# Four of sixteen scale and shift columns of a hybrid decoder layer, computed on TensorE instead of VectorE

## The chip, the core and the metric

One core of a Trainium2 chip runs the whole layer in one launch. The metric is the device time of that launch in microseconds (us). PE is TensorE's matmul row and PEld its weight loads, DVE is VectorE, ACT is ScalarE, POOL is GpSimd, SP is SyncE, which here issues nearly all transfers.

## What is computed

The layer normalises the residual stream `x` (1024 tokens by 1024 channels), modulates it by a scale and a shift that come from a conditioning vector `c`, projects it, runs sparse attention and a state-space mixer side by side, and projects back. The change touches the modulation alone:

```python
mod = jax.nn.silu(c) @ w_ada + b_ada                # c: (1, 1024), w_ada: (1024, 3072)
shift, scale, gate = jnp.split(mod, 3, axis=-1)     # 1024 values each
h = rms_norm(x, norm_g) * (1 + scale[:, None, :]) + shift[:, None, :]
proj = h @ w_in
```

`silu(c) @ w_ada` is a product of one row with a matrix: 24 parts of 128 outputs, each over 1024 inputs. Parts 0 to 7 are the shift, 8 to 15 the scale, 16 to 23 the gate.

## The kernel before

**The parts of the modulation.** `mod_chunk(j)` (L230) loads 128 rows of the transposed `w_ada` (512 KB: one output on each partition, its 1024 weights along it) into a `w4` buffer and forms the sum on DVE: one `scalar_tensor_tensor` (the helper at L148) multiplies the tile by `sc` and adds up along the partition into one column of `macc`. `sc` holds `2 * silu(c)` copied to all 128 partitions; `sc_half` (L222) makes it from a 4 KB row by products with a column of ones (L224), a tanh on ACT (L225) and a step on DVE. The steps `ma0` to `ma7` are parts 8 to 15 (scale), `mb0` to `mb7` parts 0 to 7 (shift), `mod0` to `mod7` parts 16 to 23 (gate, needed much later).

**From the parts to h.** `mod_cols(k)` (step `mc{k}`, L286) turns the columns 8+k and k of `macc` into `gs` and `sh`, the gain and the shift of the 128 channels of block k. Meanwhile the tokens are prepared in two halves of 512: squares and their sums (`sq0` to `sq7`, the table `FLG` puts `sq0` and `sq3` on DVE, L148, the others on ACT, L242), the root (`rstd0`, `rstd1`: eleven small DVE instructions), the scaling of x (`xsc0`, `xsc1`: two tiles on DVE at L155, two on ACT at L257), and transposes on PE into PSUM (`xb{k}{half}`, L265, two buffers of tag `pv`). `h_chunk` (step `h{k}{half}`, L290) then runs two ACT instructions on that PSUM tile (L296), once into `hhi` in a reduced format, once into `hf` in full, and the remainder `hlo = hf - hhi` is formed on DVE, on POOL or by an accumulating transfer (L300). The sixteen h steps feed the first projections on PE: `kva{k}` (L330 to L332, three products per tile: high times high, high times low, low times high) and `u{k}m` (L351), which accumulate over k. `kvaw{k}` loads and splits the weights of `kva`: a cast on ACT (L208), a subtraction on DVE or POOL.

**Order.** A list of step names, `ORD`, gives the order in which the steps are written down. Its head is `sc1 sc0 lb pu xl_0 sq0 sq2 sq1 sq3 ma7 mb4 ma0 rstd0 mb0 kvaw0 ma5 xl_1 xsc0 sq5 xb10 sq4 xb00 sq6 sq7 mg mc0 h00 mb2 rstd1 xsc1 ma1 kvaw1 mb1 mc1 mb3 ma2 mc2 kvaw5 mb6 ...`. The context `in_order` (L170) pins that order on DVE and ACT up to the step `eo`, and on SP up to `sw`; what is written after `eo` may be placed earlier by the framework's scheduler where it finds an engine free, and PE and POOL are not pinned at all. Within an engine the program that comes out is fixed and is executed strictly in its order.

**Buffers.** `w4` has 19 buffers of 4 KB a partition and serves the weight tiles of `w_ada`, the squares' scrap tiles and the projection weights; SP holds back a load until the buffer it was given is released. In PSUM the tag `mm` has two buffers; the step `pu` takes both at the start for the accumulators `pu0` of `u{k}m`.

Of the kernel before, what the change touches and what calls it, by code (L numbers as in the profile page):

```python
# [26 lines left out]
ORD = """
sc1 sc0 lb pu xl_0 sq0 sq2 sq1 sq3 ma7 mb4 ma0 rstd0 mb0 kvaw0 ma5 xl_1 xsc0 sq5 xb10 sq4 xb00 sq6 sq7 mg mc0 h00 mb2
rstd1 xsc1 ma1 kvaw1 mb1 mc1 mb3 ma2 mc2 kvaw5 mb6 xb01 kvaw2 ma3 mc3 h01 xb20 mb5 eo kvaw4 mb7 h10 xb30 cU1 cz4 cU0
h20 xb21 h30 kvaw3 xb11 h11 h21 xb31 kvaw6 xb40 h31 ma4 s5l mc4 h40 xb70 mc7 ll h70 xb50 u0m u1m ma6 u2m mc5 h50 kva0  # L30
mc6 kva1 xb51 kva2 u3m xb61 xb60 h51 h61 xb71 h60 kva3 xb41 tb h41 kva4 kvaw7 h71 s5p u4m kva5 kva6 u5m kva7 u6m sw
tabf kpa0 kpa1 cKC kpan0 kvb0 kvb1 kvb2 prep0 kvb3 kvb4 kvb5 u7m u0 cU2 kvb6 mats0 xl0 kpat0 tab0 prep1 scan0 kpan1 u1
cU3 mats1 kpat1 xl1 kvb7 kpb0 tq kpb1 kpbn0 u2 qaw0 u3 mod0 mod1 out0 prep2 tab1 cVC kpbn1 scan1 out1 tab2 xl2 cmpk
qaw1 cmpv kpbt0 qaw2 qa0 mod2 mod3 mod4 mats2 hidk qaw3 qaw4 qaw5 qa1 qa2 kpbt1 qa3 qa4 qa5 mod5 qaw6 qa6 mod6 qaw7
qa7 qp0 qp1 qpn0 qs0 prep3 qpn1 qs1 tab3 hidv xl3 qw0 scan2 qr0 cz0 mats3 qw1 scan3 qb0 qb1 gw gates mod7 modf cok cov
cmpK qb2 scalev qb3 z0_0 z0_1 qb4 z0_2 qt01 qb5 qb6 qb7 out2 cz2 qr1 qt00 g2 cz1 z0_3 qpb0 qpb1 qpbn0 ca0 z0_4 qpbn1
z0_5 z0_6 z0_7 out3 cz3 kt ha00 ha01 hs01 hb00 hc00 ha02 z1_0 z1_1 z1_2 ha03 hs03 hb01 hb02 z1_3 z1_4 qsb0 z1_5 z1_6
hc01 ha04 qt10 ha05 hs05 hb03 hc02 hc03 hb04 hb05 z1_7 hc04 hc05 z2_0 yp00 z2_1 qsb1 ca1 ha06 ha07 hs07 hb06 z2_2 z2_3
z2_4 hb07 ct0 hc06 ha10 z2_5 hc07 z2_6 ub00 qt11 z2_7 ub01 ha11 hs11 hb10 hb11 ub02 z3_0 z3_1 z3_2 hc10 hc11 yp01 ha12
ha13 ub03 qw2 ct1 z3_3 qr2 ub04 ub05 ha14 ub06 ha15 cz5 z3_4 z3_5 ub07 ub10 z3_6 z3_7 hs15 hs13 hb12 hb13 z4_0 hb14  # L40
hb15 qt20 ub11 ha16 ha17 hc12 hc13 hc14 yp02 z4_1 z4_2 qt21 ub12 hs17 hb16 ha20 ha21 hb17 z4_3 ca2 hc15 hs21 ha22 z4_4
ha23 hc16 z4_5 z4_6 z4_7 hb20 ub13 cz6 hb21 hc17 hs23 hc20 yp03 ub14 yp10 z5_0 z5_1 z5_2 hb22 z5_3 qw3 qr3 ub15 hc21
z5_4 cz7 z5_5 z5_6 ha24 hb23 ha25 ub16 ub17 hs25 hb24 z6_0 z5_7 hc22 hc23 hc24 ha26 ha27 ct2 hs27 z6_1 z6_2 qt30 z6_3
z6_4 z6_5 z6_6 yp11 z6_7 yp12 hb25 hb26 hc25 ha30 qt31 ha31 ha32 ha33 hs31 hs33 ca3 hb27 hb30 z7_0 ub20 hc26 hb31 glul
z7_1 z7_2 z7_3 hb32 hc27 z7_4 z7_5 hc30 hc31 hc32 ha34 hb33 yp13 ub21 qw7 ha35 hs35 z7_6 z7_7 sp hc33 ct3 glu00 grow
ha36 ha37 glu03 qr7 qt70 hb34 hc34 glu01 qt71 ha70 ub22 ub23 ub24 ub25 hb35 hc35 ub26 hs37 ub27 hb36 hc36 ca7 ha71 ct7
glu02 glu10 glu11 hs71 ub30 hb37 hb70 qw6 glu12 qr6 ha72 ub31 ub32 ub33 hc37 hc70 at0 ha73 hs73 glu13 wo10 wo11 hb71
hc71 hb72 hc72 ha74 hb73 wo12 wo13 ub34 ub35 ub36 ha75 hc73 qt60 ub37 ub70 hs75 ha76 hb74 hb75 ha77 hs77 ub71 so0 so1
qt61 hc74 hc75 hb76 hb77 ca6 ub72 hc76 hc77 ha60 ha61 ct6 qw5 hs61 ub73 hb60 hc60 ub74 hb61 ha62 ha63 so2 hs63 qr5
hb62 ub75 ha64 hc61 hc62 hb63 ha65 ub76 hs65 hb64 hb65 ha66 ha67 so4 ub77 ca5 ub60 ub61 hc63 hc64 so5 qt50 ha50 qt51  # L50
ub62 hs67 hb66 hb67 hc65 qw4 qr4 ub63 so7 hc66 ha51 hs51 hc67 ub64 hb50 hb51 hc50 hc51 so6 ha52 ha53 ha54 ha55 ha56
hs53 ub65 hb52 hb53 ub66 so3 wo00 wo01 wo02 wo03 ct5 hc52 qt41 at3 hc53 ub67 ub50 hs55 hb54 hb55 hc54 ha57 hs57 ca4
ao30 hc55 hb56 hb57 ao31 ao00 ao01 qt40 at1 ha40 at2 ao10 ha41 hc56 hs41 hb40 hb41 hc57 hc40 ha42 ub51 ao11 ha43 ub52
ao20 hs43 hb42 hb43 ct4 hc41 hc42 ao21 ub53 ub54 ha44 ha45 at7 ub55 ub56 ub57 ao70 hc43 hs45 hb44 hb45 ao71 ha46 ub40
at5 at6 ha47 hc44 ao50 ao51 ao61 hs47 hc45 hb46 hc46 hb47 ao60 ub41 ub42 ub43 hc47 ub44 ub45 ub46 ub47
""".split()
FLG = dict(
    cw1280="d", cw1408="d", cw1536="d", cw1664="d", cw1816="d", cw1944="d", cw2072="d", cw2200="d", cw2328="d",
    cw2456="d", cw512="d", cw640="d", h00="p", h01="d", h10="p", h11="t", h20="p", h21="d", h30="d", h31="d", h40="d",
    h41="t", h50="t", h51="t", h60="d", h61="d", h70="t", h71="d", kw0="p", kw1="d", kw2="p", kw3="d", kw4="d",  # L60
    kw5="p", kw6="p", kw7="d", prep0="d", prep1="p", prep2="p", prep3="d", pw0="d", pw1="d", pw2="d", pw3="d",
    qw0="d", qw1="d", qw2="d", qw3="d", qw4="d", qw5="d", qw6="t", qw7="d", sq0="d", sq1="a", sq2="a", sq3="d",
    sq4="a", sq5="a", sq6="a", sq7="a", tab0="d", tab1="d", tab2="d", tab3="d", tabf="d", so0="p", at0="p", ao00="d",
    ao01="d", so1="d", at1="p", ao10="d", ao11="d", so2="p", at2="p", ao20="d", ao21="d", so3="d", at3="p", ao30="d",
    ao31="d", so4="d", ao40="d", ao41="d", so5="d", at5="p", ao50="d", ao51="d", so6="d", at6="p", ao60="d", ao61="d",
    so7="p", at7="d", ao70="d", ao71="d", wo00="d", wo01="d", wo02="d", wo03="d", wo10="d", wo11="d", wo12="d",
    wo13="d", xa0="d", xa1="d", xa2="t", xa3="d", xa4="d", xa5="d", xa6="d", xa7="d")
# [1552 lines left out]
```

## Time and profile before

| | |
|---|---|
| time, median of 3 runs | 692.42 us (692.40 to 692.64) |
| the profiled execution: its own time | 691.38 us |
| the profiled execution: span from first to last instruction | 689.5 us |
| PE busy | 623.5 us, 90% of the span |
| DVE busy | 567.3 us, 82% |
| ACT busy | 377.9 us, 55% |
| POOL busy | 148.6 us, 22% |
| granted TensorE clock, mean over the span | 0.980 |

The profile is of one execution. A busy share is a mean over stages with different limits, so the stage that the change touches (the first 60 us or so) is read by itself: the engines' instructions in order of time, with the idle time ahead of each and what ended it.

### The profile page before, as it was taken

The page shows a single profiled execution, that of the slowest core. Times are in us where ns is not written, and L with a number is a line of the kernel's source. Part 1 is how long each engine was busy: PE and PEld are TensorE (multiplying, and loading weights), DVE is VectorE, ACT ScalarE, POOL GpSimd, SP SyncE. Part 2 cuts the span into 40 slices and gives each one's busy share as a digit, 9 for nine tenths or more (in the row PEclk, how much of TensorE's full clock was granted, in tenths as well). Part 3 has the DMA queues.
Part 4 walks back from the last instruction along what each step waited for, and adds up shares of the span by engine and source line. Part 5 has one row for each costly group of instructions (what it writes and reads, how often), then busy time and mean ns, then how long its engine had stood idle before and what let it go on. Part 6 is the DMA issues. An engine that isn't in the chain of part 4 may idle for free.

```text
span 689.5 us, 12618 instructions
## 1 busy us (share of the span) xinstructions
PE 623.5 (90%) x4662; PEld 492.1 (71%) x4662; DVE 567.3 (82%) x1106; ACT 377.9 (55%) x732; POOL 148.6 (22%) x159
## 2 busy tenths in 40 slices
PE   2478999999698999999999999989899999799996
PEld 0356787788587886888788887556677777687775
DVE  5998999777937889876677787998898998998872
ACT  3677413735162252555586786547756855756640
POOL 0153209147232020640011101132001220011010
PEclk9989999999899999999999999999999999999999
DMA  8975211355276624373656868499689599688994
GB/s 319 417 246 104 47 62 41 115 158 136 64 246 199 212 68 109 83 231 94 131 139 154 207 186 183 124 207 208 183 172 206 132 226 222 184 215 213 224 222 86
DMA packets 209759, 116.76 MB, mean 169 GB/s; under 512 B 159073, under 2 KB 188513, under 8 KB 209698
## 3 DMA queue, kind: packets, MB, share of 16 engines
q1 hardware_dynamic: 205858, 109.38, 61.5%
...
q14 instruction: 24, 0.20, 0.1%
...
## 4 chain that ended last, share of the span: by engine, by line
PE 41%; DVE 21%; issue 5%; ACT 4%; DMA 2%; SPq 1%; POOL 1%; DVEq 0%; ACTq 0%; POOLq 0%
PE pcp L351 9%; PE po L1053 8%; PE S L1170 7%; DVE hl L148 4%; PE po L1263 3%; PE pglu L1015 3%; DVE st L1187 3%; PE ptp L331 2%; PE ptp L332 2%; PE ptp L330 1%; DVE ps L151 1%; ACT pp L1203 1%; DVE z L151 1%; PE pg L530 1%; PE ph L901 1%
## 5 line engine op out<-in xcount | busy, mean ns | idle before, releaser
L1203 ACT ACTIVATE pp<-S,st 128x640 f32<-128x640 f32 (+7 forms) x128 | 88.6, 699 | 60.5 <-DVE st L1187 46.5
L148 DVE SCALAR_TENSOR_TENSOR hl<-pp,st,hl 128x640 f16<-128x640 f32 (+7 forms) x128 | 100.5, 817 | 4.9 <-ACT hl L1222 4.8
L1222 ACT ACTIVATE hl<-pp,st 128x640 f16<-128x640 f32 (+7 forms) x128 | 85.2, 728 | 8.2 <-DVE st L151 7.1
L1053 PE MATMUL po<-wo,oh 128*128 128x512 f32 x264 | 85.2, 407 | 3.7 <-DVE wo L151 2.4
L351 PE MATMUL pcp<-hhi,wh 128*128 128x512 f32 x208 | 84.8, 408 | 0.0
L351 PE MATMUL pcp<-hhi,wl 128*128 128x512 f32 x208 | 82.6, 397 | 0.0
L351 PE MATMUL pcp<-hlo,wh 128*128 128x512 f32 x208 | 82.4, 396 | 0.0
L1187 DVE TENSOR_REDUCE st<-S 128x1 f32<-128x1024 f32 (+3 forms) x64 | 57.5, 916 | 6.9 <-PE S L1170 6.7
L1170 PE MATMUL S<-kT,qh 128*128 128x128 f32 (+3 forms) x192 | 60.7, 375 | 1.0 <-ACT pp L1203 0.7
L1053 PEld LDWEIGHTS po<-wo,oh 128*128 128x128 f32 x264 | 48.7, 191 | 14.9 <-DVE wo L151 3.8
L330 PE MATMUL ptp<-wsp,hhi 128*128 128x512 f32 x128 | 53.5, 420 | 6.5 <-ACT hhi L296 4.1
L1263 PE MATMUL po<-V,PT 128*128 128x64 f16 x1584 | 59.0, 193 | 0.0
L1263 PEld LDWEIGHTS <-PT 128*128 128x128 f16 x1584 | 54.0, 98 | 5.7 <-issue 5.1
L1170 PE MATMUL S<-kT,ql 128*128 128x128 f32 (+3 forms) x192 | 55.3, 346 | 0.1
L332 PE MATMUL ptp<-wsp,hlo 128*128 128x512 f32 x128 | 53.0, 416 | 1.5 <-POOL hlo L151 1.5
L331 PE MATMUL ptp<-wsp,hhi 128*128 128x512 f32 x128 | 53.5, 418 | 0.5 <-DVE wsp L151 0.5
L151 POOL TENSOR_TENSOR qr<-ropeb 128x512 f32<-128x512 f32 x16 | 23.5, 1488 | 121.7 <-DVE ropeb L151 69.7
L1053 PE MATMUL po<-wo,ol 128*128 128x512 f32 x120 | 47.9, 402 | 0.8 <-DVE ol L151 0.8
L1170 PEld LDWEIGHTS S<-kT,qh 128*128 128x128 f32 x192 | 33.7, 193 | 17.2 <-issue 11.8
L351 PEld LDWEIGHTS pcp<-hlo,wh 128*128 128x128 f32 x208 | 39.1, 188 | 9.2
L351 PEld LDWEIGHTS pcp<-hhi,wh 128*128 128x128 f32 x208 | 39.2, 189 | 8.3
L351 PEld LDWEIGHTS pcp<-hhi,wl 128*128 128x128 f32 x208 | 39.2, 188 | 8.1
...
## 6 DMA issues: line engine op xcount, KB each, us to landing
...
```

Of the source, the lines that this page charges most:

```text
L148: dve.scalar_tensor_tensor(out=o, in0=a, scalar=s, in1=b, op0=o0, op1=o1, **kw)
L151: e.tensor_tensor(out=o, in0=a, in1=b, op=op)
L330: pe.matmul(p, H(k)[:, tsl], w[:, 0, :], start=k == 0, stop=False)
L331: pe.matmul(p, H(k)[:, tsl], w[:, 1, :], start=False, stop=False)
L332: pe.matmul(p, H(k, True)[:, tsl], w[:, 0, :], start=False, stop=k == 7)
L351: pe.matmul(p[:], w[:, k, :], H(k, l)[:, halves(half)], start=(k == 0 and w is hi and not l), stop=(k == 7 and l))
L1053: pe.matmul(p, a[x][:, k, :], w[y][:, halves(n)], start=k == 0 and m == 0, stop=k == 3 and m == 2)
L1170: pe.matmul(R[:, c0:c1], w, x, start=bank not in opened, stop=False, skip_group_check=True)
L1187: dve.tensor_reduce(out=st[br], in_=us[br][0][:, :W], axis=AX.X, op=OP.max, negate=True)
L1203: act.activation(pp[:, :W], R[:, :W], AF.Exp, bias=st[br], accum_out=st4[:, 1, 2 * (h % 2) + br:2 * (h % 2) + br + 1])
L1222: act.activation(hl[:, :W], pp[:, :W], AF.Copy, scale=st[br])
L1263: pe.matmul(o, p, v, start=first, stop=end, skip_group_check=True)
```

## The change

Parts 0, 8, 9 and 10 (`mb0`, `ma0`, `ma1`, `ma2`) leave DVE. For them the weights are loaded in their natural layout (128 inputs on the partitions, eight blocks of them along it, 128 outputs each; again 512 KB), and PE forms the 128 outputs as a column: eight accumulating products with a 128x128 block as the stationary operand and one column of `scc` as the moving one, straight into column 0 of a PSUM tile (tag `mm`). `scc` is `2 * silu(c)` with the inputs on partitions, 128x8; a new step `scc` loads `c` once more in that layout (4 KB), runs a tanh on ACT and one step on DVE. `scc` lies in columns 16 to 23 of `macc`, which the gate parts overwrite later. `mod_cols` reads its column from PSUM for these four parts. In `ORD` the new step stands third, between `sc0` and `lb`, and `pu` moves from fifth place to just ahead of `u0m`; all else keeps its place. (All marks `mp0` to `mp15` but 0, 8, 9 and 10 say `d`, DVE.)

```diff
-sc1 sc0 lb pu xl_0 sq0 sq2 ...
+sc1 sc0 scc lb xl_0 sq0 sq2 ... ll h70 xb50 pu u0m u1m ma6 ...
+    mp0="p", mp1="d", ... mp8="p", mp9="p", mp10="p", mp11="d", ...
+    scc = macc[:, 16:24]
+    MP = {}
+
+    def sc_cols():
+        cT = w2([128, 8], F32, "cT")
+        dma(cT[:], t["cT"])
+        act.activation(scc, cT[:], AF.Tanh, scale=0.5)
+        stt(scc, scc, 1.0, cT[:], OP.add, OP.mult)
+
+    def mod_col(j):
+
+        return MP.pop(j)[:, 0:1] if j in MP else macc[:, j:j + 1]
+
     def mod_chunk(j):
         w = w4([128, 1024], F32, "wada")
+        if FLG.get(f"mp{j}", "d") == "p":
+            dma(w[:], t["w_adaN"][j], "m")
+            p = MP[j] = pmm("pmod")
+            for k in range(8):
+                pe.matmul(p[:, 0:1], w[:, 128 * k:128 * k + 128], scc[:, k:k + 1], start=k == 0, stop=k == 7)
+            return
         dma(w[:], t["w_adaT"][j * 128:(j + 1) * 128, :], "m")
         stt(w[:], w[:], 1.0, sc[:], OP.mult, OP.mult, accum_out=macc[:, j:j + 1])
...
     def mod_cols(k):
-        ts(dve, gs[:, k:k + 1], macc[:, 8 + k:9 + k], hng[:, 0, k:k + 1], hng[:, 1, k:k + 1], OP.mult, OP.add)
-        ts(dve, sh[:, k:k + 1], macc[:, k:k + 1], 0.5, bada[:, k:k + 1], OP.mult, OP.add)
+        ts(dve, gs[:, k:k + 1], mod_col(8 + k), hng[:, 0, k:k + 1], hng[:, 1, k:k + 1], OP.mult, OP.add)
+        ts(dve, sh[:, k:k + 1], mod_col(k), 0.5, bada[:, k:k + 1], OP.mult, OP.add)
...
+    I("scc")(sc_cols)
...
+    a["w_adaN"] = g("w_ada")[:, :2048].reshape(8, 128, 16, 128).transpose(2, 1, 0, 3).reshape(16, 128, 1024)
+    a["cT"] = np.asarray(inputs["c"])[0].reshape(8, 128).T
```

## Rows read from the trace of the kernel before

**Rows 1.** Busy time by stretch: width, then PE, PEld, DVE, ACT, POOL, clock, DMA.
```profile
22.00:56.50 34.50, 23.68 (x88) 16.04 (x86) 31.06 (x64) 24.83 (x37) 12.23 (x8) 0.90 0.87 295
56.50:178.00 121.50, 119.14 (x612) 96.46 (x613) 105.23 (x315) 56.70 (x97) 51.98 (x57) 1.00 0.34 92
```

**Rows 2.** Transfers, 0 to 60 us: DMA busy tenths in 40 slices of 1.5 us.
```profile
DMA  0489999999999999999999999995018879987051
```

**Rows 3.** SP's issues in order of time (start, duration, engine), and bada's landing.
```profile
3.45 0.74 SPq L140 DMA_DIRECT2D bada<-in_b_ada_dram  x1
...
DMA to landing us min/median/max: 7.1/7.1/7.1
```

**Rows 4.** DVE in order of time; in brackets the idle time before and its end.
```profile
7.36 1.22 DVE L148 SCALAR_TENSOR_TENSOR sq<-x 128x1024 f32<-128x1024 f32 x1
...
10.41 1.23 DVE L148 SCALAR_TENSOR_TENSOR sq<-x 128x1024 f32<-128x1024 f32 x1 [1.83 <-DMA x<-in_x_dram]
...
11.84 1.23 DVE L148 SCALAR_TENSOR_TENSOR wada<-wada,sc 128x1024 f32<-128x1024 f32 x1 [0.19 <-DMA wada<-in_w_adaT_dram]
...
14.38 1.22 DVE L148 SCALAR_TENSOR_TENSOR wada<-wada,sc 128x1024 f32<-128x1024 f32 x1
...
15.53 0.17 DVE L157 TENSOR_SCALAR vtmp<-ss 128x4 f32<-128x4 f32 x1
...
24.13 1.23 DVE L148 SCALAR_TENSOR_TENSOR wada<-wada,sc 128x1024 f32<-128x1024 f32 x1 [0.95 <-DMA wada<-in_w_adaT_dram]
...
29.75 1.22 DVE L148 SCALAR_TENSOR_TENSOR wada<-wada,sc 128x1024 f32<-128x1024 f32 x1
...
31.20 0.69 DVE L151 TENSOR_TENSOR wsp<-wraw,wsp 128x512 fp32r<-128x512 f32 x1 [0.23 <-ACT wsp L208]
...
34.41 1.22 DVE L148 SCALAR_TENSOR_TENSOR wada<-wada,sc 128x1024 f32<-128x1024 f32 x1
```

**Rows 5.** ACT in order of time.
```profile
18.72 2.19 ACT L257 ACTIVATE x<-x,rstd 128x1024 f32<-128x1024 f32 x2 [2.06 <-DVE rstd L148]
...
24.88 0.19 ACT L242 ACTIVATION_READ_ACCUMULATOR sq<-x 128x1 f32 x1
24.97 0.76 ACT L296 ACTIVATE hhi<-ptr,sh,gs 128x512 fp32r<-128x512 f32 x1
...
30.57 0.60 ACT L208 CAST wsp<-wraw 128x512 fp32r<-128x512 f32 x1
33.39 0.78 ACT L296 ACTIVATE hhi<-ptr,sh,gs 128x512 fp32r<-128x512 f32 x1 [2.21 <-DVE sh L157]
```

**Rows 6.** PE in order of time.
```profile
21.63 1.99 PE L265 MATMUL ptr<-ident,x 128*128 128x128 f32 x8 [15.55 <-DVE x L155]
...
27.83 0.79 PE L332 MATMUL ptp<-wsp,hlo 128*128 128x512 f32 x1 [0.82 <-POOL hlo L151]
...
34.22 0.68 PE L330 MATMUL ptp<-wsp,hhi 128*128 128x512 f32 x1 [1.94 <-ACT hhi L296]
...
36.59 1.12 PE L265 MATMUL ptr<-ident,x 128*128 128x128 f32 x4 [0.41 <-ACT hf L296]
...
41.21 0.79 PE L332 MATMUL ptp<-wsp,hlo 128*128 128x512 f32 x1 [0.64 <-POOL hlo L151]
```

**Rows 7.** PE at 56 us, in order of time.
```profile
56.57 0.50 PE L351 MATMUL pu<-hlo,wh 128*128 128x512 f32 x1 [1.57 <-DMA hlo<-hf]
```

**Rows 8.** The product with the ones (L224): count, duration ns min/median/max, start.
```profile
L224 PE MATMUL pcb<-cr,ones x4: 1056/1056/1187, 2.3 to 5.0; 1*128 1x512 f32 x4
```

**Rows 9.** Full-format products of 128 columns on PE, in order of time.
```profile
186.37 0.64 PE L852 MATMUL py<-s5X,s5T 128*128 128x128 f32 x2
186.80 0.63 PE L853 MATMUL py<-z,s5CA 128*128 128x127 f32 x2
...
198.72 0.23 PE L780 MATMUL pk<-s5c,BD 128*48 128x16 f32 x2
198.79 0.37 PE L782 MATMUL pk<-s5CA,BD 128*48 128x112 f32 x2
```

More of the change, by code (lines that the diff above doesn't have):

```diff
@@ L27 @@
 ORD = """
[L28 to L52, printed above, removed]
@@ L53 @@
-ao30 hc55 hb56 hb57 ao31 ao00 ao01 qt40 at1 ha40 at2 ao10 ha41 hc56 hs41 hb40 hb41 hc57 hc40 ha42 ub51 ao11 ha43 ub52
-ao20 hs43 hb42 hb43 ct4 hc41 hc42 ao21 ub53 ub54 ha44 ha45 at7 ub55 ub56 ub57 ao70 hc43 hs45 hb44 hb45 ao71 ha46 ub40
-at5 at6 ha47 hc44 ao50 ao51 ao61 hs47 hc45 hb46 hc46 hb47 ao60 ub41 ub42 ub43 hc47 ub44 ub45 ub46 ub47
+sc1 sc0 scc lb xl_0 sq0 sq2 sq1 sq3 ma7 mb4 ma0 rstd0 mb0 kvaw0 ma5 xl_1 xsc0 sq5 xb10 sq4 xb00 sq6 sq7 mg mc0 h00 mb2 rstd1 xsc1 ma1 kvaw1 mb1 mc1 mb3 ma2 mc2 kvaw5 mb6 xb01 kvaw2 ma3 mc3 h01 xb20 mb5 eo kvaw4 mb7 h10 xb30 cU1 cz4 cU0 h20 xb21 h30 kvaw3 xb11 h11 h21 xb31 kvaw6 xb40 h31 ma4 s5l mc4 h40 xb70 mc7 ll h70 xb50 pu u0m u1m ma6 u2m mc5 h50 kva0 mc6 kva1 xb51 kva2 u3m xb61 xb60 h51 h61 xb71 h60 kva3 xb41 tb h41 kva4 kvaw7 h71 s5p u4m kva5 kva6 u5m kva7 u6m sw tabf kpa0 kpa1 cKC kpan0 kvb0 kvb1 kvb2 prep0 kvb3 kvb4 kvb5 u7m u0 cU2 kvb6 mats0 xl0 kpat0 tab0 prep1 scan0 kpan1 u1 cU3 mats1 kpat1 xl1 kvb7 kpb0 tq kpb1 kpbn0 u2 qaw0 u3 mod0 mod1 out0 prep2 tab1 cVC kpbn1 scan1 out1 tab2 xl2 cmpk qaw1 cmpv kpbt0 qaw2 qa0 mod2 mod3 mod4 mats2 hidk qaw3 qaw4 qaw5 qa1 qa2 kpbt1 qa3 qa4 qa5 mod5 qaw6 qa6 mod6 qaw7 qa7 qp0 qp1 qpn0 qs0 prep3 qpn1 qs1 tab3 hidv xl3 qw0 scan2 qr0 cz0 mats3 qw1 scan3 qb0 qb1 gw gates mod7 modf cok cov cmpK qb2 scalev qb3 z0_0 z0_1 qb4 z0_2 qt01 qb5 qb6 qb7 out2 cz2 qr1 qt00 g2 cz1 z0_3 qpb0 qpb1 qpbn0 ca0 z0_4 qpbn1 z0_5 z0_6 z0_7 out3 cz3 kt ha00 ha01 hs01 hb00 hc00 ha02 z1_0 z1_1 z1_2 ha03 hs03 hb01 hb02 z1_3 z1_4 qsb0 z1_5 z1_6 hc01 ha04 qt10 ha05 hs05 hb03 hc02 hc03 hb04 hb05 z1_7 hc04 hc05 z2_0 yp00 z2_1 qsb1 ca1 ha06 ha07 hs07 hb06 z2_2 z2_3 z2_4 hb07 ct0 hc06 ha10 z2_5 hc07 z2_6 ub00 qt11 z2_7 ub01 ha11 hs11 hb10 hb11 ub02 z3_0 z3_1 z3_2 hc10 hc11 yp01 ha12 ha13 ub03 qw2 ct1 z3_3 qr2 ub04 ub05 ha14 ub06 ha15 cz5 z3_4 z3_5 ub07 ub10 z3_6 z3_7 hs15 hs13 hb12 hb13 z4_0 hb14 hb15 qt20 ub11 ha16 ha17 hc12 hc13 hc14 yp02 z4_1 z4_2 qt21 ub12 hs17 hb16 ha20 ha21 hb17 z4_3 ca2 hc15 hs21 ha22 z4_4 ha23 hc16 z4_5 z4_6 z4_7 hb20 ub13 cz6 hb21 hc17 hs23 hc20 yp03 ub14 yp10 z5_0 z5_1 z5_2 hb22 z5_3 qw3 qr3 ub15 hc21 z5_4 cz7 z5_5 z5_6 ha24 hb23 ha25 ub16 ub17 hs25 hb24 z6_0 z5_7 hc22 hc23 hc24 ha26 ha27 ct2 hs27 z6_1 z6_2 qt30 z6_3 z6_4 z6_5 z6_6 yp11 z6_7 yp12 hb25 hb26 hc25 ha30 qt31 ha31 ha32 ha33 hs31 hs33 ca3 hb27 hb30 z7_0 ub20 hc26 hb31 glul z7_1 z7_2 z7_3 hb32 hc27 z7_4 z7_5 hc30 hc31 hc32 ha34 hb33 yp13 ub21 qw7 ha35 hs35 z7_6 z7_7 sp hc33 ct3 glu00 grow ha36 ha37 glu03 qr7 qt70 hb34 hc34 glu01 qt71 ha70 ub22 ub23 ub24 ub25 hb35 hc35 ub26 hs37 ub27 hb36 hc36 ca7 ha71 ct7 glu02 glu10 glu11 hs71 ub30 hb37 hb70 qw6 glu12 qr6 ha72 ub31 ub32 ub33 hc37 hc70 at0 ha73 hs73 glu13 wo10 wo11 hb71 hc71 hb72 hc72 ha74 hb73 wo12 wo13 ub34 ub35 ub36 ha75 hc73 qt60 ub37 ub70 hs75 ha76 hb74 hb75 ha77 hs77 ub71 so0 so1 qt61 hc74 hc75 hb76 hb77 ca6 ub72 hc76 hc77 ha60 ha61 ct6 qw5 hs61 ub73 hb60 hc60 ub74 hb61 ha62 ha63 so2 hs63 qr5 hb62 ub75 ha64 hc61 hc62 hb63 ha65 ub76 hs65 hb64 hb65 ha66 ha67 so4 ub77 ca5 ub60 ub61 hc63 hc64 so5 qt50 ha50 qt51 ub62 hs67 hb66 hb67 hc65 qw4 qr4 ub63 so7 hc66 ha51 hs51 hc67 ub64 hb50 hb51 hc50 hc51 so6 ha52 ha53 ha54 ha55 ha56 hs53 ub65 hb52 hb53 ub66 so3 wo00 wo01 wo02 wo03 ct5 hc52 qt41 at3 hc53 ub67 ub50 hs55 hb54 hb55 hc54 ha57 hs57 ca4 ao30 hc55 hb56 hb57 ao31 ao00 ao01 qt40 at1 ha40 at2 ao10 ha41 hc56 hs41 hb40 hb41 hc57 hc40 ha42 ub51 ao11 ha43 ub52 ao20 hs43 hb42 hb43 ct4 hc41 hc42 ao21 ub53 ub54 ha44 ha45 at7 ub55 ub56 ub57 ao70 hc43 hs45 hb44 hb45 ao71 ha46 ub40 at5 at6 ha47 hc44 ao50 ao51 ao61 hs47 hc45 hb46 hc46 hb47 ao60 ub41 ub42 ub43 hc47 ub44 ub45 ub46 ub47
@@ L56 @@
 """.split()
 FLG = dict(
[L58 to L62, printed above, removed]
@@ L1370, in hymba @@
             I(f"xb{k}{h}", f"xsc{h}")(lambda k=k, h=h: x_block(h, k))
-        I(f"ma{k}", "sc0", "sc1")(lambda k=k: mod_chunk(8 + k))
-        I(f"mb{k}", "sc0", "sc1")(lambda k=k: mod_chunk(k))
+        I(f"ma{k}", "sc0", "sc1", "scc")(lambda k=k: mod_chunk(8 + k))
+        I(f"mb{k}", "sc0", "sc1", "scc")(lambda k=k: mod_chunk(k))
         I(f"mc{k}", "mg", f"ma{k}", f"mb{k}")(lambda k=k: mod_cols(k))
```

6 lines of the change are left out of this document (1 added, 5 removed).

## The prediction

> **What bounds the kernel now.** I read the views in this order: busy time by stretch, the transfers' busy slices, then DVE, ACT and PE in order of time over the first 60 us, because only there does the change touch an instruction. The stretches show two regimes. From 56.5 to 178 us PE is busy 119.1 of 121.5 us at full granted clock [rows 1]: its total work sets the pace there, and a time gained or lost before 56.5 us is passed on nearly whole. Before it nothing is full: DVE is the busiest with 31.1 of 34.5 us, PE has 23.7, ACT 24.8 [rows 1]. So the question is what sets the moment at which PE becomes dense, 56.57 us [rows 7], and whether DVE, which loses work, is in it.
>
> Followed back by waits it is a chain with little DVE in it. PE starts there on an `hlo` that a transfer brought. Earlier, ACT begins the h step of block 1 at 33.39 us after 2.21 us of waiting for `sh` from DVE [rows 5]. DVE got there by way of a wait for ACT's cast, done 31.17 us [rows 4, 5], which stood behind ACT's scaling of the second half of x, which stood behind `rstd1`, which DVE began right after the part `mb2`; and `mb2` began at 24.13 us after 0.95 us of waiting for its weights [rows 4]. The transfers are at 9 tenths or more in every slice from 4.5 to 37.5 us [rows 2]. So in the first 24 us the transfers set the pace, and DVE has time that it then spends waiting.
>
> **The change part by part.**
>
> *The new step `scc`.* Its 4 KB load is issued where `bada` was, right behind four tiles of x. `bada` was issued at 3.45 us and landed 7.1 us later, at 10.55 [rows 3], just after the last x tile, at 10.41 [rows 4]; I take 10.5 for the new load. The order of DVE and ACT is pinned here, so behind the wait stand on DVE the square `sq0`, which began at 7.36 [rows 4], and on ACT two squares. The tanh and the DVE step on 8 columns are not in the trace; together they cost at least 0.36 us (a four-column step on DVE takes 0.17 [rows 4], ACT's read of its sums 0.19 [rows 5]) and at most 1.3 (0.69 and 0.60 on 512 columns [rows 4, 5]); eight columns are nearest to the small ones, so 0.5 with the hand-over. DVE then starts its squares at 11.0. Two full-tile products take 1.15 us each from start to start (14.38 to 15.53) [rows 4], so `ma7` starts at 13.3 where it started at 11.84: 1.5 us late. The old 1.83 us of waiting for x is swallowed in this.
>
> *Parts 8 and 0 leave DVE* (`ma0`, `mb0`). Each takes 1.15 us off. `ma0` stood ahead of `rstd0`: 1.5 less 1.15 leaves `rstd0` 0.35 late, ACT's scaling (which waited for it until 18.72) and its four squares as late, the last ending at 25.4 instead of 25.07 [rows 5]. `mb0` stood ahead of work that then runs into the wall of `mb2`'s weights at 24.13: it buys nothing; without that wall it would be worth up to the 0.95 us of that wait. `rstd1` waits for the later of ACT's squares (25.4) and `mb2` (25.3 and the new transfer's share): it starts some 0.2 us late. On PE both products fall into the 15.55 us of idleness ahead of 21.63 [rows 6]: nothing.
>
> *Part 9 leaves DVE* (`ma1`, at 29.75). Behind it DVE wants `wsp`, for which it waited until 31.20 on ACT [rows 4]; so the hole only becomes longer: nothing. *Part 10* (`ma2`, 34.41): DVE runs 1.15 us ahead from there. No row of PE up to 41.21 waits for DVE [rows 6], and at 56.57 PE waits for a transfer [rows 7]: I take nothing, and at best the 1.57 us of that wait.
>
> *Parts 9 and 10 on PE.* Each full-format product is two instructions: the two products with the ones appear as four [rows 8]. So a part is 8 times 2, 16 pairs of a weight load and a one-column product. Such a pair isn't in the trace. Above it stands the pair with 128 moving columns at the slower of the two paces that PE shows, 0.43 us for two, 0.214 each; below it the one with 48 weight columns and 16 moving ones at the faster pace, 0.07 for two, 0.035 each [rows 9]. It has the weights of the first and the columns of the second; I take the middle, 0.125: 2.0 us a part (0.6 to 3.4), 4.0 for both. They need weights that land at about 25 and 28 us and PSUM columns that `mc0` has released, so they run between 25 and 36 us. There PE is idle 0.82, 1.94 and 0.41 us [rows 6], 3.2 in all. 0.8 is left over and delays the transposes at 36.59, for whose result ACT waits; the next wait, 0.64 us for POOL at 41.21, gives most of it back: plus 0.2 (0 to 3.0).
>
> Here a rule speaks against the change. The Trainium skill ("FP8 and Floating Point Precision", section TensorE Precision Notes) counts four passes through the array for a true 32-bit product. By that a part would be twice as long and the sum would come out beyond the slower rival below. The trace has two instructions a product, not four [rows 8], and I follow the trace.
>
> *The clock.* In the stretch before 56.5 us the granted clock is 0.90 on the mean [rows 1], against 1.00 after it. More products on PE may raise it; all of it would be worth a tenth of 23.7 us, 2.4. I take nothing.
>
> *SP, buffers, `pu`.* SP issues one transfer more, 0.45 to 0.74 us [rows 3], while four x tiles keep the transfers full: nothing but its share of bandwidth. The four tiles are released by PE instead of DVE, not later. `pu` takes the `mm` buffers after `mc2`, and its first product comes long after: nothing. ACT has one small instruction more.
>
> **Sum.** Plus 0.2 at `rstd1`, plus 0.2 on PE: 0.4 us later at 56.57, passed on. The profiled execution's own time, 691.38 us, becomes 691.8; the median of the runs lies 1.04 us above that execution, and the forecast is for the median: 692.42 + 0.4 = 692.8.
>
> **The rivals.**
>
> *DVE is the bound after all.* For: it is the busiest engine in the stretch, 31.1 of 34.5 us [rows 1], and the waits are short; four products of 1.15 us less make 4.6, of which the late start takes 1.5 and the new step 0.2; 2.9 are left: 689.5. It would need the wall of `mb2`'s weights to move with it, or the scheduler to fill the holes with later work, which it is free to do past `eo`. Against: the wall at 24.13 and the cast at 31.17. That PE gains its clock would give about the same, up to 2.4 us: 690.0.
>
> *PE becomes the bound of the first stage (slower).* If a pair costs the 0.214 us of the upper row, parts 9 and 10 take 6.8 us of PE in a stretch that has 3.2 free; 3.6 are left over and stand, in PE's fixed order, ahead of the transposes that ACT waits for; 0.6 comes back at 41.21: plus 3.0 and 0.2, 695.6. It decides from 1.9 us a part on. For: PE does wait on ACT and ACT on PE in turn there, so a late transpose is late work for both. Against: the long moving side is absent. A variant of it: if a product were four pairs, at the 0.125 taken above, a part would take 4.0 us, the two 8.0, 8.0 less 3.2 and 0.6 leaves 4.2, with the late start's 0.2 4.4: 696.8; the two instructions of [rows 8] speak against it, and it gets 0.03. (It is what the Trainium skill's page on precision, named above, would make of the change.)
>
> *The load of `scc` isn't behind x and the start isn't late, or the change only moves holes.* If `scc` comes by 7.4 us, `rstd0` is 1.15 us early, but `mb2`'s weights still hold the rest: 692.6, inside the forecast.
>
> *The order is reshuffled.* What stands behind `eo`, and all of PE and POOL, is placed anew; a transfer or a step that comes at another place costs or gives what one wait of this stage is, 1.5 to 3 us: 690 or 695.
>
> **How the numbers follow.** About 0.2% (1.4 us) is what a measurement of this kernel can tell from no change. Forecast with the third rival: 0.40, all of it within. DVE as the bound 0.20, the clock 0.06, a lucky order 0.07: 0.33, faster. PE as the bound 0.15, its variant 0.03, an unlucky order 0.09: 0.27, slower. The range reaches to both: 688.5, where DVE's gain has a microsecond of the clock with it, to 696.0, a little past the slower rival.
>
> **What would show it.** `ma7`'s product should start near 13.3 us, with DVE waiting for ACT ahead of its first square for some 3.5 us. `mb2` should still wait for its weights, for longer than 0.95. The 64 new product instructions should take 6 to 11 us in all, the first half before 21 us. PE should become dense within a microsecond of 56.57. If the prediction is wrong, ACT's h step of block 1 (33.39 us) will have moved by more than 0.5 us, or PE's dense stretch will start well before or after its old place while that step has not moved.

## The result, and the profile after

| | before | after |
|---|---|---|
| median of the first series | 693.86 us (10 runs) | 700.74 us (10 runs) |
| ratio, 95% interval | | 1.0086 (1.0067 to 1.0105): +6.0 us |
| two more series | | 1.0046 (1.0017 to 1.0075): +3.2 us; 1.0079 (1.0051 to 1.0107): +5.5 us |
| profiled execution: its time, span | 691.38, 689.5 us | 701.84, 700.0 us |
| PE busy / DVE busy in the span | 623.5 / 567.3 us | 637.1 / 561.7 us |

The ratio, and the microseconds that stand beside it, are an estimate from all runs of a series; they are not the difference of the two medians (6.9 us in the first series). The change costs 3 to 6 us, 4.9 on the mean of three series. The forecast was +0.4, and the range ended at +3.6. (It started from a median of three runs, 692.42; the ten runs of the series have 693.86.) Executions of one and the same kernel differ by several us (before: 688.2 to 698.2), so a difference of the two profiled executions alone (10.5 us) is no measure, and medians of a series are good to about 2 us.

First the start. SP's issues in order of time (start, duration, engine, operation), before:

```profile
4.72 0.65 SPq L140 DMA_DIRECT2D pos<-in_pos_k_dram  x1
5.42 0.47 SPq L140 DMA_DIRECT2D pos<-in_pos_v_dram  x1
6.45 4.29 SPq L140 DMA_DIRECT2D wada<-in_w_adaT_dram  x4
10.78 0.43 SPq L140 DMA_DIRECT2D wraw<-in_w_in_dram  x1
11.25 0.43 SPq L140 DMA_DIRECT2D w2s<-in_w_k_dram  x1
```

and after, with the transfers' busy tenths from 0 to 60 us in 40 slices, to be laid beside [rows 2]:

```profile
3.46 0.65 SPq L104 DMA_DIRECT2D cT<-in_cT_dram  x1
...
5.62 0.90 SPq L104 DMA_DIRECT2D pos<-in_pos_v_dram  x1
6.71 0.39 SPq L104 DMA_DIRECT2D w2s<-in_w_k_dram  x1
8.85 0.37 SPq L104 DMA_DIRECT2D w2s<-in_w_v_dram  x1
10.16 0.82 SPq L104 DMA_DIRECT2D wada<-in_w_adaT_dram  x2
11.03 0.91 SPq L104 DMA_DIRECT2D wada<-in_w_adaN_dram  x2
```
```profile
DMA  0489993499999999999999999996971006887898
```

The two loads of `w2s`, 64 KB each and needed only after 200 us, now stand ahead of the weights, and the first weights leave 3.7 us later. While SP waits, the transfers run dry: slices 7 and 8 (9 to 12 us) show 3 and 4 tenths where [rows 2] has nines.

Then DVE, ACT and PE of after in order of time; in brackets the idle time ahead and what ended it:

```profile
10.58 0.17 DVE L112 SCALAR_TENSOR_TENSOR macc<-macc,cT 128x8 f32<-128x8 f32 x1 [3.08 <-ACT macc L201]
...
27.07 1.23 DVE L112 SCALAR_TENSOR_TENSOR wada<-wada,sc 128x1024 f32<-128x1024 f32 x1 [1.81 <-DMA wada<-in_w_adaT_dram]
...
42.19 0.28 DVE L121 TENSOR_SCALAR gs<-pmod,mod 128x1 f32<-128x1 f32 x1 [4.60 <-PE pmod L214]
```
```profile
10.34 0.21 ACT L201 ACTIVATE macc<-cT 128x8 f32<-128x8 f32 x1 [3.56 <-DMA cT<-in_cT_dram]
...
19.49 0.62 ACT L172 CAST wsp<-wraw 128x512 fp32r<-128x512 f32 x1 [6.85 <-DMA wraw<-in_w_in_dram]
20.01 2.19 ACT L241 ACTIVATE x<-x,rstd 128x1024 f32<-128x1024 f32 x2
...
27.48 0.77 ACT L280 ACTIVATE hhi<-ptr,sh,gs 128x512 fp32r<-128x512 f32 x1
...
39.25 0.78 ACT L280 ACTIVATE hhi<-ptr,sh,gs 128x512 fp32r<-128x512 f32 x1 [0.95 <-PE ptr L249]
...
43.19 0.78 ACT L280 ACTIVATE hhi<-ptr,sh,gs 128x512 fp32r<-128x512 f32 x1 [2.49 <-PE ptr L249]
```
```profile
17.68 6.96 PE L214 MATMUL pmod<-macc,wada 128*128 128x1 f32 x32 [11.53 <-DVE rstd L112]
24.49 1.95 PE L249 MATMUL ptr<-ident,x 128*128 128x128 f32 x8
...
32.61 3.41 PE L214 MATMUL pmod<-macc,wada 128*128 128x1 f32 x16
...
38.16 1.05 PE L249 MATMUL ptr<-ident,x 128*128 128x128 f32 x4
...
39.87 2.29 PE L214 MATMUL pmod<-macc,wada 128*128 128x1 f32 x16
...
42.56 0.60 PE L249 MATMUL ptr<-ident,x 128*128 128x128 f32 x4
...
61.59 0.80 PE L335 MATMUL pu<-hlo,wh 128*128 128x512 f32 x1 [2.46 <-DMA hlo<-hf]
```

The two ACT rows of before that answer to those at 39.25 and 43.19:

```profile
35.09 0.78 ACT L296 ACTIVATE hhi<-ptr,sh,gs 128x512 fp32r<-128x512 f32 x1
...
37.75 0.78 ACT L296 ACTIVATE hhi<-ptr,sh,gs 128x512 fp32r<-128x512 f32 x1 [1.21 <-PE ptr L265]
```

Three things are to be seen. `mb2` starts at 27.07 us in place of 24.13 [rows 4]. The new products take 3.48 us each for parts 8 and 0, 3.41 for part 9 and 2.29 for part 10. DVE stands 4.60 us in front of the column of part 10, but that is not what ACT waits for: its two waits behind these products, 0.95 and 2.49 us, in before 0 and 1.21, were ended by the transposes (`ptr`), which stand behind the products in PE's order; the column had been used at 42.19, the transposes started at 42.56. And PE's wait for the `hlo` of [rows 7] is 2.46 us in place of 1.57; behind it the granted clock falls. By stretch (width, PE, PEld, DVE, ACT, POOL, clock, DMA), after; the first row is to be laid beside [rows 1]:

```profile
22.00:56.50 34.50, 28.50 (x121) 23.37 (x121) 25.61 (x55) 23.73 (x37) 8.04 (x6) 0.95 0.83 294
56.00:60.00 4.00, 3.02 (x14) 2.19 (x14) 3.49 (x7) 2.67 (x5) 2.10 (x2) 1.00 0.93 244
60.00:64.00 4.00, 2.42 (x6) 1.94 (x7) 3.69 (x26) 2.12 (x3) 0.91 (x1) 0.66 0.33 91
```

The first h step is 2.5 us late (27.48, before 24.97 [rows 5]), the last one 6.4 (74.7, before 68.3), the last product for U 6.4 (105.4, before 99.0), the last store of the output 10.6.

### The profile page after: what moved, and what is told of

Same layout as the page of the kernel before. It is cut to its first block, busy times and chain, and to the rows that moved or that the text cites. A ratio compares the mean times of both kernels' runs of the same rounds, so it can differ in the third digit from the quotient of the medians.

```text
span 700.0 us, 12747 instructions
## 1 busy us (share of the span) xinstructions
PE 637.1 (91%) x4726; PEld 507.7 (73%) x4726; DVE 561.7 (80%) x1099; ACT 379.0 (54%) x733; POOL 145.3 (21%) x159
## 4 chain that ended last, share of the span: by engine, by line
PE 41%; DVE 21%; ACT 5%; issue 5%; DMA 2%; SPq 1%; DVEq 0%; ACTq 0%
PE pcp L335 11%; PE po L1037 9%; PE S L1154 7%; DVE hl L112 5%; PE po L1247 3%; DVE st L1171 3%; DVE ps L115 2%; PE ptp L316 1%; PE ptp L315 1%; ACT pp L1187 1%; PE ptp L314 1%; DVE o L115 1%; DMA zz<-zsd 1%; DVE z L115 1%; PE pg L514 1%
## 5 line engine op out<-in xcount | busy, mean ns | idle before, releaser
L115 POOL TENSOR_TENSOR qr<-ropeb 128x512 f32<-128x512 f32 x16 | 24.2, 1534 | 124.2 <-DVE ropeb L115 71.1
```

Source lines behind the costliest of these rows:

```text
L115: e.tensor_tensor(out=o, in0=a, in1=b, op=op)
```

## Theories and the table of runs

Four theories: **start** (the extra load and the two early `w2s` loads make the weights late), **price** (the products of parts 9 and 10 stand in PE's fixed order ahead of what DVE and ACT wait for), **order** (something else was placed anew), and **relief** (DVE's freed time is worth something that the other three hide). The order theory could be looked at in the programs themselves: compared engine by engine, PE has before's sequence with the four groups of products put in, DVE before's with four products out and one step in (a step of 0.2 us changes places with its neighbour), ACT one step more, POOL no difference, and SP differs only within its first loads. No later step was moved.

All runs, with the start of the first h step, the start of the last product for U ("the end of the U products" in the expectations) and PE's wait for that `hlo` in the profiled execution, and the time against before in the same series:

| version | first h | last U | wait for hlo | ratio (95%) | us |
|---|---|---|---|---|---|
| before | 25.0 | 99.0 | 1.57 | | |
| before_again | 24.8 | 98.7 | 1.38 | 0.9995 (0.9972 to 1.0019) | -0.3 |
| pu_late | 24.9 | 100.5 | 2.26 | 0.9990 (0.9961 to 1.0019) | -0.7 |
| packed_none | 24.6 | 98.7 | 1.16 | 0.9998 (0.9974 to 1.0021) | -0.1 |
| no_parts | 27.6 | 101.0 | 0.61 | 0.9998 (0.9974 to 1.0022) | -0.1 |
| no_parts_2 | 27.0 | 100.3 | 0.28 | 1.0017 (0.9990 to 1.0045) | +1.2 |
| packed_two | 24.5 | 100.4 | 1.94 | 1.0032 (1.0004 to 1.0060) | +2.2 |
| packed_two_2 | 24.2 | 100.2 | 1.96 | 1.0020 (0.9994 to 1.0047) | +1.4 |
| two_parts | 27.0 | 103.1 | 1.83 | 1.0038 (1.0011 to 1.0065) | +2.6 |
| packed | 24.8 | 102.4 | 2.06 | 1.0026 (0.9996 to 1.0057) | +1.8 |
| packed_2 | 24.2 | 100.4 | 1.96 | 1.0046 (1.0012 to 1.0080) | +3.2 |
| pinned | 25.3 | 103.0 | none | 1.0055 (1.0022 to 1.0088) | +3.8 |
| after | 27.5 | 105.4 | 2.46 | 1.0086 (1.0067 to 1.0105) | +6.0 |
| four_again | 26.3 | 102.0 | 1.59 | 1.0046 (1.0017 to 1.0075) | +3.2 |
| four_third | 26.2 | 103.9 | 2.36 | 1.0079 (1.0051 to 1.0107) | +5.5 |
| one_910 | 24.4 | 100.1 | 1.94 | 0.9989 (0.9961 to 1.0017) | -0.8 |
| twice_910 | 24.5 | 108.7 | none | 1.0130 (1.0097 to 1.0163) | +9.0 |
| twice_80 | 29.6 | 102.8 | 0.76 | 1.0058 (1.0032 to 1.0084) | +4.0 |
| delayed | 29.6 | 103.4 | 1.48 | 1.0060 (1.0030 to 1.0090) | +4.2 |
| best_b | 24.2 | 98.8 | 1.17 | 1.0035 (1.0013 to 1.0057) | +2.4 |

## Experiments

**How much of a late first stage arrives at the end: delayed.** To before, one line:

```diff
+    x_load(1)
     x_load(0)
```

> The kernel before with the four tiles of the second half of x loaded once more ahead of the first half: 2 MB, some 5 us of transfers, and nothing else. It measures how much of a late start arrives at the end. If PE's dense stretch passes it on whole: hhi's first step, the end of the U products and the time all +5 us. If part of it is taken up later: the anchors shift by 5 us as far as the stage that takes it up, and the time by less; the version that kept the late start but no product (+2.0 us at the end of the U products, 0 in the median) would expect +3 or less.

The first h step came 4.6 us late, the last U product 4.0 us behind 99.4 (the mean of the three executions with before's instruction order, before, before_again and pu_late), and the time rose by 4.2 us (2.1 to 6.2). So most of a late first stage arrives at the end, and within the noise all of it. Over the whole table the last U product less 99.4 follows the time within some 2 us, best_b (-0.6 against +2.4) excepted; that product is read from one execution of each version, the time from a series.

**The change once more: four_again and four_third.** No edit.

> The changed kernel again, on the chip that the next three run on. Both theories expect what was measured: the ratio to before near 1.009, some 6 us. In its profile the second weight part for DVE behind the first x half (mb2) starts near 27.1 us and DVE waits some 4.6 us for pmod ahead of 42.2 us.

> The changed kernel a third time. It was +6.0 us in its first series and +3.2 in the second, and its two profiles differ at the end of the U products (105.4 and 102.0): in the slower one PE waited 2.46 us for hlo near 61.6 us and the granted clock fell to 0.66 behind it, in the other 1.59 us at 1.00. If that wait decides: the executions fall into two groups, near 695 and near 700 us, and the profile's end of the U products is near 102 or near 105 with the wait below 1.7 or above 1.9 us.

+3.2 and +5.5 us. In four_again `mb2` started at 25.90 and in four_third at 25.82 us, not at 27.07, so the start of the first profile was an unlucky one. The two groups near 695 and 700 us show in the second series (eight executions up to 696.8, four from 698.9 on), less clearly in the third. That the clock goes with the wait for `hlo` shows in PE's rows of four_again:

```profile
38.17 1.84 PE L214 MATMUL pmod<-macc,wada 128*128 128x1 f32 x16
...
59.55 0.50 PE L335 MATMUL pu<-hlo,wh 128*128 128x512 f32 x1 [1.59 <-DMA hlo<-hf]
59.89 0.39 PE L335 MATMUL pu<-hhi,wh 128*128 128x512 f32 x1
60.12 0.40 PE L335 MATMUL pu<-hhi,wl 128*128 128x512 f32 x1
```

After 1.59 us of waiting, products of 0.40 us; in the first profile, after 2.46 us, of 0.80.

**The start: two_parts, packed_two, packed, no_parts, packed_none, pinned.** two_parts and no_parts are the changed kernel with two and no parts on PE:

```diff
-    mp9="p", mp10="p"          # no_parts: mp0 and mp8 too
+    mp9="d", mp10="d"
```

The packed versions bring the columns of `c` in with the identity, so that SP issues no load more:

```diff
-    ident = load("ident", [128, 128], t["ident"])
+    identc = load("ident", [128, 152], t["ident"])
+    ident, macc = identc[:, 0:128], identc[:, 128:152]
...
-        dma(cT[:], t["cT"])
-        act.activation(scc, cT[:], AF.Tanh, scale=0.5)
-        stt(scc, scc, 1.0, cT[:], OP.add, OP.mult)
+        act.activation(cT[:], scc, AF.Tanh, scale=0.5)
+        stt(scc, cT[:], 1.0, scc, OP.add, OP.mult)
```

pinned keeps the extra load and adds a dependency that holds each `w2s` load behind the first load of `wraw`.

> The changed kernel with only parts 8 and 0 as products; 9 and 10 are back on DVE. Start theory (the load of the columns and the two w2 loads ahead of the weights cost the start some 3 us, the products little): mb2 stays near 27.1 us, the time stays within 1 us of the changed kernel, +5 to +6 us against before. Price theory (a pair of 0.217 us makes parts 9 and 10 stand in PE's way): DVE's wait of 4.6 us for pmod near 42 us is gone and with it some 3 to 4 us; +2 to +3 us against before remain, those of the start. Order theory (the new place of the first U product and the like cost the time, not these): +6 us as with four parts.

> The changed kernel with four parts as products, but the 8 columns of c ride in the load of the identity, so that SP issues no transfer more than before and its order of loads is that of before (weights ahead of the two w2 loads). Start theory: mb2 back at 24.1 us or earlier, the first square near 7.4, and 3 us or more of the 6 are gone: 0 to +3 us against before. Price theory: the start is back, but parts 9 and 10 still hold DVE for some 4 us near 40 us: +3 to +4 us. Order theory: +6 us still.

> Both at once: the columns of c in the load of the identity, and only parts 8 and 0 as products. If start and price are the whole loss, nothing of it remains: within 1 us of before. If DVE's freed 2.3 us were worth anything without the two costs, it is faster than before by 1 to 2 us. Order theory: still +4 to +6 us.

> The changed kernel with all sixteen parts on DVE again, but the new step and its load kept (its columns are then used by nothing). Start theory: mb2 near 27 us and DVE without its relief, so the end of the U products at least 2.7 us behind the 99.0 of before, and +3 us in the time. If the products are the whole loss: 0 us. If the relief of DVE was worth something that the start hid, it is slower than the version with parts 8 and 0 by up to 2.3 us.

> No product, columns of c in the load of the identity: of the change only the two small instructions on ACT and DVE, the place of the first U product and whatever the scheduler puts elsewhere remain. Start and price theories: 0 us against before. Order theory: what remains of the loss in the version with two parts and this load (+1.4 us at the end of the U products, some 2 us in the time) is here too.

> The changed kernel with its four parts and its own load of the columns, but the two w2 loads held behind the first load of w_in, where they were before; one transfer more than before still stands ahead of the weights. Start theory, as eight transfers in flight: the weights' first load is issued near 7 us in place of 10.16, mb2 starts within 0.6 us of 24.1 to 24.7, and the time is that of the version with the columns in the identity's load, +1.5 to +3 us. If the load of the columns itself (and the wait of DVE for it until 10.6 us) is the cost: mb2 stays behind 26 us, and the time at +3 to +6 us.

The packed versions and pinned have before's order of loads again, no dry slices, and `mb2` at 23.8 to 24.9 us. DVE in packed:

```profile
24.41 1.23 DVE L112 SCALAR_TENSOR_TENSOR wada<-wada,sc 128x1024 f32<-128x1024 f32 x1 [2.23 <-DMA wada<-in_w_adaT_dram]
...
39.42 0.28 DVE L121 TENSOR_SCALAR gs<-pmod,mod 128x1 f32<-128x1 f32 x1 [4.50 <-PE pmod L213]
```

So the late start comes from the two `w2s` loads ahead of the weights: in pinned the load of `cT` is there, and the first h step is 25.3. What the late start is worth is smaller than its 2 us at the first h step: the version with it and no product has the last U product 1.6 and 0.9 us behind 99.4, and the time at -0.1 and, once more with the same kernel, +1.2 us (-0.7 to 3.1):

> The version with the late start and no product on PE, once more, since its anchor (+2.0 us at the end of the U products) and its median (0) contradict each other. If an early delay is passed on, as in the kernel with the doubled load (+4.4 us at that anchor, +4.2 in the time): +1.5 to +3 us. If a late start alone is taken up somewhere: within 1 us of before again.

I put it at 0 to 2 us, not settled closer (the mean of the change's three series less that of packed and packed_2 would leave 2.4). packed_none, with no product and no late start, is at -0.1 us (-1.8 to 1.5): tanh, the extra DVE step and the rest cost nothing that shows. With the start mended and all four parts on PE, packed, packed_2 and pinned still lose 1.8, 3.2 and 3.8 us, 2.9 on the mean of a loss of 4.9: the products are the larger part.

**The price: one_910, twice_910.** packed, with one product in place of eight for parts 9 and 10 (the rest of these two sums is left out), or with the eight made twice:

```diff
-            for k in range(8):
+            n = 1 if j in (9, 10) else 8        # twice_910: 16 turns over the same 8 blocks
+            for k in range(n):
```

> The version with the columns in the identity's load and all four parts on PE, but of the eight products of part 9 and of part 10 only the first is made: the rest of these two sums is left out (the output is another one for it), place and order stay. Price theory: the wait of 4.5 us on DVE for pmod near 39 us shrinks to under 2 us, the products of parts 9 and 10 take 0.5 to 0.9 us together in place of 5.6, the last h step comes 2 us earlier (69.7 in place of 71.7), the time is 2 us under that of the full version. Placement theory (having them on PE at all costs, not how long they take): no change against it, +2 us against before.

> The same version with the eight products of parts 9 and 10 each made twice (the second pass starts the sum anew): 5.6 us more on PE in front of what follows. Price theory: the last h step 4 to 6 us behind 71.7, the time 4 to 6 us above the full version, +6 to +8 us against before. Placement theory: within 1 us of the full version.

> All four parts on PE, columns in the identity's load, once more beside it. Price theory: 1.5 to 3 us behind the version with parts 8 and 0 alone, for the 4.5 us that DVE waits for parts 9 and 10 near 39 us, so +2 to +4 us against before; first series +1.8 with an interval from -0.3 to 4.0.

The late parts' products took 0.70, 5.60 and 13.65 us of PE; DVE's wait for the column of part 10 was 0.61, 4.50 and 9.13 us; the last h step came at 69.4, 71.7 and 77.7 us; the time was -0.8, +1.8 (in the second series +3.2) and +9.0 us. The price theory's numbers held, but for a doubling that cost 7.2 us above packed (5.8 above packed_2) where 4 to 6 were expected. PE, DVE and ACT of twice_910:

```profile
29.63 6.83 PE L214 MATMUL pmod<-ident,wada 128*128 128x1 f32 x32
...
40.30 6.82 PE L214 MATMUL pmod<-ident,wada 128*128 128x1 f32 x32
```
```profile
36.49 0.28 DVE L121 TENSOR_SCALAR gs<-pmod,mod 128x1 f32<-128x1 f32 x1 [3.36 <-PE pmod L214]
...
47.16 0.28 DVE L121 TENSOR_SCALAR gs<-pmod,mod 128x1 f32<-128x1 f32 x1 [9.13 <-PE pmod L214]
```
```profile
36.93 0.78 ACT L280 ACTIVATE hhi<-ptr,sh,gs 128x512 fp32r<-128x512 f32 x1 [5.66 <-DVE sh L121]
...
49.08 0.78 ACT L280 ACTIVATE hhi<-ptr,sh,gs 128x512 fp32r<-128x512 f32 x1 [7.94 <-PE ptr L249]
```

The price reaches ACT by two ways. Doubled, part 9 holds DVE, and ACT's h step of block 1 waits 5.66 us for `sh`; behind part 10 ACT waits 7.94 us for the transposes that stand behind the products on PE. Made once, as in packed, the products cost by the second way: ACT waits 0.96 and 2.40 us for transposes behind parts 9 and 10, where packed_two has 0 and 1.21, and DVE's 4.50 us make neither ACT nor PE wait for DVE any longer than in packed_two, up to PE's wait for `hlo`. (In four_again and packed_2 one wait of ACT for DVE's `sh`, 0.33 us, stands behind part 10; packed_two has 0.70 at that place.)

**The early parts: twice_80, packed_two_2.** packed_two with the products of 8 and 0 made twice, by the same edit.

> The columns in the identity's load, only parts 8 and 0 on PE, and their products made twice: 14 us of them instead of 7, from 14.2 us on, so that PE's transposes of x start near 28.2 instead of 21.3 us. If PE's place ahead of the transposes is free only as long as they are not ready: first h step +6.5 us or more, and +4 to +6 us in the time. If something else than PE sets the first stage: under +2 us.

> Parts 8 and 0 alone on PE, columns in the identity's load, once more: +2.2 us in its first series, while the version that makes these two parts in full and one product of 9 and of 10 was at -0.8. Its profile showed the first h step 0.5 us earlier than before and the end of the U products +1.4, behind a wait of 1.94 us for hlo. If parts 8 and 0 cost nothing on PE, as they end before the transposes are ready: within 1 us of before, and the end of the U products within 1 us of 99.4, the mean of the three profiles with before's order, unless the wait for hlo is above 1.8. If they do cost: +1.5 to +3 us again.

Doubled, they occupy PE from 14.02 to 27.80 us, the first h step is 4.7 us late (expected 6.5; in before ACT's squares held it until 24.97 anyway, 1.4 us beyond the end of the transposes) and the time +4.0. Made once, they end at 21.2 as the transposes become ready, and the first h step is 0.5 to 0.8 us earlier than before. Yet the time was +2.2 and +1.4 us, and +2.6 in two_parts; one_910, which has these two parts in full, was at -0.8. By the mean of packed_two, packed_two_2 and one_910 they cost 0.9 us; with intervals that reach from -2.7 to 4.2 it isn't settled that they cost anything. A place for it does show. PE in packed_two:

```profile
56.40 0.50 PE L334 MATMUL pu<-hlo,wh 128*128 128x512 f32 x1 [1.94 <-DMA hlo<-hf]
56.74 0.42 PE L334 MATMUL pu<-hhi,wh 128*128 128x512 f32 x1
56.97 0.62 PE L334 MATMUL pu<-hhi,wl 128*128 128x512 f32 x1
57.38 0.63 PE L334 MATMUL pu<-hlo,wh 128*128 128x512 f32 x1
```

The transfer of this `hlo` was issued at 48.91 us, before at 49.46; it let PE go on at 56.40, before at 56.57 [rows 7]. Over the eight executions that have neither a late start nor the late parts in full (before, before_again, pu_late, packed_none, packed_two, packed_two_2, one_910, best_b) the issue lies between 48.6 and 49.7 and that product between 56.1 and 56.6. So who comes earlier waits longer, and in packed_two, packed_two_2 and one_910 the clock falls behind the wait. ACT gets its next transposes then, 62.41 us where before had 61.05.

**Order: pu_late and before_again.** before, with `pu` moved in `ORD` as the change moves it:

```diff
-sc1 sc0 lb pu xl_0 ...
+sc1 sc0 lb xl_0 ... ll h70 xb50 pu u0m
```

> The kernel before with one step moved: the first U product is listed where the change lists it, behind the h step of block 5. Order theory: +2 us or more, with PE's wait for hlo near 57 us at 2 us or more and a granted clock below 0.7 in the 4 us behind it. Other theories: 0 us, that wait near 1.6 us and the clock at 1.00.

> The kernel before, unchanged, for a second profile of it: how far one execution's anchors lie from another's. Expected: time 0 against before; mb2 within 0.5 us of 24.1, the wait for hlo near 57 us between 1.4 and 1.9 us, the end of the U products within 1 us of 99.0, and differences of up to 3 us behind that, since the first profile was 2.5 us under its median.

The move leaves every engine's instruction order as it was, so pu_late is one more execution of before, and its time says so (-0.7). Its profile is the instructive one: wait for `hlo` 2.26 us, granted clock 0.57 in the 4 us behind it, last U product 1.5 us behind before's. So the longer wait with the slower clock behind it comes without any change too, in one of the four profiles that have no product on PE and no late start; of the four profiles with parts 8 and 0 in full on PE, no late part in full and before's DVE order (packed_two, packed_two_2, one_910, two_parts), all four have it. That the longer wait is what makes the clock fall is read from such pairs; no run changes the wait alone.

**DVE's freed time put to use: best_b.** packed_two, with one square moved to DVE, `mb2` behind `rstd1` and `pu` back:

```diff
-sq5="a"   ... mb2 rstd1 xsc1 ...
+sq5="d"   ... rstd1 mb2 xsc1 ...
```

> Parts 8 and 0 on PE, the columns in the identity's load, DVE's freed time put to use: one square of the second half of x (sq5) moves from ACT to DVE, mb2 moves behind rstd1, and the first U product back to its old place. If what ended last ahead of rstd1 was the wait for mb2's weights (24.1 us) and ACT's squares (24.6): rstd1 starts about 1 us earlier, ACT scales the second half of x near 27.3 in place of 28.5, and the time is 1 us under before, if the wait for hlo stays under 1.9 us. If the arrival of x's second half sets it: 0.

`rstd1` did start about 1 us earlier (24.32, behind ACT's squares, for 25.24 in packed_two) and ACT scaled at 27.60 for 28.56. But its next h step waited for `sh` of DVE, now later in DVE's order, and started at 33.27, against 33.47 there. The last U product was at 98.8, the time at +2.4 us (0.9 to 4.0). No version beat before by more than the noise, so no run shows a use of DVE's freed time, and where best_b loses behind 99 us was not found.

## Why the prediction was wrong, point by point

- **The landing of `scc`: right.** It came at 10.3 (forecast 10.5), DVE went on at 10.7 (11.0), `ma7` started at 13.50 (13.3). The last of these is partly luck: DVE was free at 13.04, earlier than forecast, and then waited 0.46 us for the late weights.
- **`rstd0` and ACT behind it: the step is wrong in what it waits for.** DVE had `rstd0` ready at 18.16, before ACT could use it: ACT stood until 19.49 on the cast of `wraw`, which was late with all weights. ACT scaled at 20.01, not at 18.72 plus 0.35.
- **"SP issues one transfer more ... nothing but its share of bandwidth": this step failed.** SP's queue is a term of the sum: with the new load in it the scheduler put two unneeded loads ahead of the weights, which the prediction's list of what stays had not covered. `mb2` started 2.9 us late (1.8 and 1.7 in the later profiles) and not at 24.13, where the prediction left it. Worth 0 to 2 us at the end. (A misreading beside it changes nothing: the nines of [rows 2] reach to 40.5 us, not 37.5.)
- **Parts 9 and 10 at 0.125 us a pair: the mis-sized term.** Measured 0.213 to 0.217 for parts 8, 0 and 9, and 0.115 to 0.213 for part 10. The prediction weighed weight size against column count and took the middle of the two rows of [rows 9], though one of them ran at the slower and the other at the faster pace. At the slower pace the upper row was right, 0.214, although 127 of its 128 moving columns were gone; the 0.125 is near the 0.115 of part 10 in four_again, at the faster pace, and that is luck. 4.0 us for parts 9 and 10 became 5.2 to 6.8.
- **The spill of 0.2 us: this step failed by its size; its way was right.** It was costed on the transposes for whose result ACT waits, and these are what ended ACT's waits of 0.95 and 2.49 us. By the prediction's own sum 5.6 us of products (packed) would leave 2.4 over and 1.8 after the 0.6 that comes back; packed less the mean of the two packed_two profiles is 2.1 at the last U product. The wait of DVE for the column, 3.6 to 5.7 us, which the prediction didn't have, took up the time that DVE had gained; ACT waited for DVE behind it for 0.33 us at most. (The next wait of PE behind 36.59 was 1.54 us for ACT at 39.25, not the 0.64 at 41.21; ACT waits for the transposes itself, so it gives nothing back: it is 1.54 again in after, at 44.69.)
- **The rival "PE becomes the bound", 0.15, was the one that came**, with its price: +3.2 forecast, of it 3.0 for the products; +1.8, +3.2 and +3.8 measured with the start mended. Its point of decision, 1.9 us a part, was passed (2.6 to 3.4 on the mean of the two parts).
- **The clock at nothing: half right.** From 22 to 56.5 us the clock row reads 0.95 in after, 0.90 before, so by that row the clock rose, as the prediction thought possible; yet part 9 ran at the slower pace and the gain did not arrive. What it didn't have is the fall to 0.66 behind the longer wait for `hlo`, some 1.5 us at the last U product (pu_late less before).
- **DVE's four products worth nothing: right.** Each hole became a wait (for `wada`, for `pmod`). The rival "DVE is the bound" fell. Of "the order is reshuffled" one case came true, two transfers at another place; no instruction on PE, ACT or POOL changed its place.
- **Two instructions a product: right.** The 32 products are 64 rows. The Trainium skill ("FP8 and Floating Point Precision", section TensorE Precision Notes) has four passes; the trace shows two instructions, and no run counts passes. What made the part cost 3.4 us was the pair's price, not their number. On the weight load the Trainium skill ("TensorE: Matmul & The Clock Gate", section LDWEIGHTS (loading the stationary operand)) gives the columns over 1.2 in ns, 107 ns for 128: the trace agrees at the faster pace (1.84 us for 16 pairs, 0.115 each) and not at the slower one (0.217).

Sum by the runs, at the last U product, as an estimate from one profile of each version; 98.9 us is the mean of before and before_again, whose clock does not fall. The late start alone is 2.1 and 1.4 us behind it (no_parts, no_parts_2). All four parts without late start and without a fall of the clock are 1.6 (packed_2). The fall is 1.6 (pu_late); packed_two, packed_two_2 and one_910 have 1.3 to 1.5 with it, so parts 8 and 0 add nothing to it here. Together 3.0 to 3.7 us without the fall and 4.3 to 5.3 with it. Measured in the three executions of the change: 3.1 (four_again, no fall), 5.0 (four_third, with it) and 6.6 (the first, with it), where `mb2` started 1.2 us later than in the other two, which no run explains.
